# Attention probabilities left undivided, with the reciprocal sums brought into the gate by way of memory

## The chip, the cores and the metric

The kernel runs on one core of a Trainium2 chip. Times are microseconds of the device for one execution. The engines are named as in the profile: PE is TensorE's matmuls, PEld its weight loads, DVE VectorE, ACT ScalarE, POOL GpSimd, and SP SyncE, which here issues all DMAs, one after the other, on a single queue.

## The reference, cut to what matters

One encoder layer over 4096 tokens of 1024 channels: a combined projection, windowed attention (8 query heads, 2 key heads, 64 channels each) beside a pooling branch, both gated, an output projection, and a norm with a residual. Of it, the change concerns the softmax and what follows it:

```python
qb = q.reshape(B, nb, BLOCK, N_KV_HEADS, Q_PER_KV, HEAD_DIM)
...
s = jnp.where(valid[None, :, None, None], s + bias[None, None], NEG)
m = jnp.maximum(jnp.max(s, axis=-1, keepdims=True), sk)
p = jnp.exp(s - m)
p = p / (jnp.sum(p, axis=-1, keepdims=True) + jnp.exp(sk - m))
o = jnp.einsum('bnkgqs,bnskd->bnqkgd', p.astype(v.dtype), vw)
...
a = banded_attention(q, k, v, rel_bias, attn_sink[l]) * jax.nn.silu(g_a)
...
mixed = jnp.einsum('bse,ed->bsd', jnp.concatenate([a, p], axis=-1), w_out[l])
```

A block has 128 queries and sees up to 384 keys: its own block and the two beside it. `sk` is a sink logit that counts in the sum and has no value.

## The kernel before

The program has two stages. The first, to about 475 us, projects the two gates and the pooling input for all tokens, in units of 512 tokens, and leaves them in DRAM. The second, which the change touches, walks the 32 blocks from the last to the first. For each unit of two blocks (256 tokens) it projects keys, values and queries, runs the attention of both blocks, multiplies it with the gate, and projects the result. Every float32 number that a matmul reads is carried as a pair of float16 numbers, a high part and the rest, so each product takes three matmuls.

A block b is handled in two **halves** of four heads. The steps of a half, with their functions:

- `scores`: PE writes four heads' scores into two PSUM tiles, `s0` and `s1`.
- `logits`, four times on DVE: adds the bias, finds the maximum, and writes the float32 tile `p` in SBUF. Its first call also has POOL copy the sink logits into the last column of `p` (the small COPY of `nsink`).
- `exps`, four times on ACT: the exponential in place, with the sum of a row into `den`. Its first call waits for that copy.
- `denominators` on DVE: scales `den` and takes the reciprocal `rd`.
- `probs`, four times on ACT: the probability p times rd, as the high float16 part `pn`; `rests`, four times on DVE: the rest.
- `turn`: one transposing DMA on SP that turns `pn` into `pt`, keys on the partitions.

When both halves are there, `values` has PE multiply `pt` with the values, and `gate` has DVE multiply the result with the gate tile `gb` (`ga_t[b]`, loaded from DRAM by `load_ga`). The names `y11`, `y12`, `y22`, `ys1` to `ys4` are the seven operands of the output projection of a unit; each is cast on ACT (`high`) and gets its rest on POOL (`low`).

What sets the order is written out by hand: each step is put into a list with a due time in us by `due` or `at_`, the list is sorted by that time, and each engine gets its instructions in the sorted order. An engine works through its own list strictly in that order: an instruction that waits holds up all behind it. The first four blocks and the last two have tables of times (`soft` and `at_`); blocks 27 to 2 are planned by a loop that takes an odd block and then the even one below it, 13 times. In the loop `softmax(b, half, t)` places a half's steps from the time t at which its scores are planned to be there.

Three queues matter for the steps below. On PE the odd part of the loop runs, in order, scores (b, 0), one output product, keys and values of the next unit, `values` of the block before, scores (b, 1), and four output products (`m22`, `m11`, `ms2`, `m12`); the even part runs scores (b, 0), queries of the next unit (first `aq`), `values`, scores (b, 1), queries (second `aq`), and two output products. The two query products use one PSUM bank in turn, so the second starts only when `keep_q` has emptied the first: a high part on ACT (`q`), then the rest on DVE. In the same way `m22` uses the bank that `keep_k` and `keep_v` (`k_all`, `vs`) have to empty.

Of the kernel before, what the change touches and what calls it, by code (L numbers as in the profile page):

```python
# [8 lines left out]
F32 = mybir.dt.float32  # L9
# [3 lines left out]
AF = mybir.ActivationFunctionType  # L13
ALU = mybir.AluOpType
# [39 lines left out]
P_SCALE = 2.0**14  # L54
# [80 lines left out]
def hybrid_layer(ctx: ExitStack, tc, io, out):  # L135
    nc = tc.nc
# [43 lines left out]
    x_scr = dram.tile([NU, P, 2, 2, HK, UT], F16, name="x_scr")  # L180
    yp_scr = dram.tile([NB, P, 4, P], F32, name="yp_scr")
    ga_scr = dram.tile([NB, P, 4, P], F32, name="ga_scr")
    wb_scr = dram.tile([6, P, 2, D], F16, name="wb_scr")
    w_scr = dram.tile([8, P, 2, HK, 512], F16, name="w_scr")

# [25 lines left out]
    with ExitStack() as actx:  # L211
# [13 lines left out]
        rows = pa.tile([P, T], F32, name="rows")  # L225
# [9 lines left out]
        def turn(name):  # L235
            turns[name] += 1
            return turns[name] % 2
# [716 lines left out]
        b = turn("n2")  # L954
        for j in range(4):
            ld(9.5 + 0.1 * j, wut[:, j], io["w_uT"][j], 0.5, w=[f"wut{j}"])
            z = turn("sq")
            for half in range(2):
                t = U0 + 4 * j + 2 * half
# [245 lines left out]
        g = 0  # L1205
# [29 lines left out]
    pb = ctx.enter_context(tc.tile_pool(name="pb", bufs=2, reuse_waits="tile"))  # L1235
    pb1 = ctx.enter_context(tc.tile_pool(name="pb1", bufs=1, reuse_waits="tile"))
# [40 lines left out]
                n += 1  # L1277

    pt, p_t, nm_t, den_t, rd_t, pn_t = {}, {}, {}, {}, {}, {}

    def keys(b):
        return [kb for kb in range(3) if 0 <= b - 1 + kb < NB]
# [6 lines left out]
    def due(t, fn, *args):  # L1289
        plan.append((t, len(plan), fn, args))  # L1290
# [30 lines left out]
    def logits(b, half, i):  # L1321

        kbs = keys(b)
        nk, lo, j0 = len(kbs) * P, kbs[0] * P, 2 * half
        if i == 0:
            nm_t[b, half] = pb.tile([P, 4], F32, name=f"nm{b}_{half}", tag="nm")
            den_t[b, half] = pb.tile([P, 4], F32, name=f"den{b}_{half}", tag="den")
            rd_t[b, half] = pb.tile([P, 4], F32, name=f"rd{b}_{half}", tag="rd")
            p = p_t[b, half] = pb.tile([P, 4, 3 * P + 1], F32, name=f"p{b}_{half}", tag="p")
            nc.gpsimd.tensor_copy(  # L1330
                p.rearrange("p (g j) k -> p g j k", g=2)[:, :, :, nk],
                nsink.rearrange("p (g j) -> p g j", g=2)[:, :, j0 : j0 + 2],
            )
        jj, gg = divmod(i, 2)
        hh, h = 2 * gg + jj, 4 * gg + j0 + jj
        nc.vector.tensor_tensor_reduce(  # L1336
            out=p_t[b, half][:, hh, :nk], in0=s_t[jj][:, gg, :nk],
            in1=bias[:, h, lo : lo + nk], scale=negc[:, h : h + 1], scalar=nsink[:, h : h + 1],
            op0=ALU.add, op1=ALU.min, accum_out=nm_t[b, half][:, hh : hh + 1],
        )  # L1340

    def exps(b, half, i):
        nk = len(keys(b)) * P
        jj, gg = divmod(i, 2)
        hh = 2 * gg + jj
        p = p_t[b, half]
        nc.scalar.activation(  # L1347
            p[:, hh, : nk + 1], p[:, hh, : nk + 1], AF.Exp, bias=nm_t[b, half][:, hh : hh + 1],
            scale=-1.0, accum_out=den_t[b, half][:, hh : hh + 1],
        )  # L1350

    def denominators(b, half):
        den = den_t.pop((b, half))
        nc.vector.tensor_scalar(
            out=den, in0=den, scalar1=1.0 / P_SCALE, scalar2=None, op0=ALU.mult
        )
        nc.vector.reciprocal(rd_t[b, half], den)

    def prob_view(b, half):
        nk = len(keys(b)) * P  # L1360
        return pn_t[b, half][:, : 8 * nk].rearrange("p (v h k) -> p v h k", v=2, h=4)

    def probs(b, half, i):
        nk = len(keys(b)) * P
        if i == 0:
            pn_t[b, half] = pb.tile(
                [P, 2 * 4 * 3 * P], F16, name=f"pn{b}_{half}", tag="pn", bufs=PN_BUFS
            )
        nc.scalar.activation(  # L1369
            prob_view(b, half)[:, 0, i], p_t[b, half][:, i, :nk], AF.Copy,  # L1370
            scale=rd_t[b, half][:, i : i + 1],
        )

    def rests(b, half, i):
        nk = len(keys(b)) * P
        pn4 = prob_view(b, half)
        nc.vector.scalar_tensor_tensor(  # L1377
            out=pn4[:, 1, i], in0=p_t[b, half][:, i, :nk], scalar=rd_t[b, half][:, i : i + 1],
            in1=pn4[:, 0, i], op0=ALU.mult, op1=ALU.subtract,
        )  # L1380

    def turn(b, half):
# [6 lines left out]
    def softmax(b, half, t):  # L1389

        for i in range(4):
            due(t + 0.1 + 0.67 * i, logits, b, half, i)
            due(t + 0.8 + 0.8 * i, exps, b, half, i)
            due(t + 4.5 + 0.6 * i, probs, b, half, i)
            due(t + 5.1 + 0.62 * i, rests, b, half, i)
        due(t + 4.3, denominators, b, half)
        due(t + 7.8, turn, b, half)


    kv_t = {}  # L1400
# [55 lines left out]
    ga_t, o_t = {}, {}  # L1456
# [244 lines left out]
    def load_gain():  # L1701
        nc.sync.dma_start(
            gpost, io["g_post"].rearrange("(o a) -> o a", o=1).to_broadcast([P, D])
        )

    now = [0.0]
    dummy = pb1.tile([P, 1], F32, name="dummy")

# [9 lines left out]
    def visit(b, half):  # L1718
        now[0] = max(now[0], free[0])
        t = max(pe(1.1, scores, b, half), free[1])  # L1720
        softmax(b, half, t)
        free[:] = t + 2.9, t + 7.9
# [71 lines left out]
    def at_(t, fn, *args):  # L1794
        due(z + t, fn, *args)

    def soft(b, half, tl, te, td, tp, tr, tt):

        for i in range(4):
            at_(tl + 0.62 * i, logits, b, half, i)  # L1800
            at_(te + 0.65 * i, exps, b, half, i)
            at_(tp + 0.55 * i, probs, b, half, i)
            at_(tr + 0.62 * i, rests, b, half, i)
        at_(td, denominators, b, half)
        at_(tt, turn, b, half)

    def cast(th, tw, u, name, f, eng):
# [11 lines left out]
    for t, fn, *args in (  # L1819
# [33 lines left out]
        at_(t, fn, *args)  # L1853

    soft(NB - 1, 0, 14.2, 14.6, 17.0, 17.6, 18.0, 20.1)
    soft(NB - 1, 1, 20.6, 21.1, 23.7, 24.2, 24.6, 26.5)
    soft(NB - 2, 0, 27.2, 27.8, 31.1, 31.6, 32.2, 34.5)
    soft(NB - 2, 1, 34.4, 35.0, 38.3, 38.8, 39.4, 41.7)
    soft(NB - 3, 0, 42.0, 42.6, 45.9, 46.4, 47.0, 49.3)
    soft(NB - 3, 1, 50.1, 50.7, 54.0, 54.5, 55.1, 57.4)  # L1860
    soft(NB - 4, 0, 59.4, 60.0, 63.2, 63.7, 64.3, 67.0)
    softmax(NB - 4, 1, 67.6)

    at_(0.0, lambda: nc.scalar.activation(dummy, mhalf, AF.Exp))
# [280 lines left out]
```

## Time and profile before

| | |
|---|---|
| median of 3 runs | 1165.77 us (1164.74 to 1165.78) |
| the profiled execution's own time | 1163.94 us |
| its span on the core | 1162.2 us |
| mean granted clock of TensorE | 0.997 |
| DMA | 228.36 MB, mean 196 GB/s |

The span runs from the first to the last instruction of the program; the execution's own time has 1.7 us more around it. All durations below come from this one execution. In the timeline a row gives the start, the duration, the engine, the line, the operation, and what was written and read; in brackets stands how long the engine had been idle and what ended that. A repeated row carries its count.

### The profile page before, as it was taken

The numbers are of one execution on the slowest core, as the hardware profiler recorded it, in microseconds if no ns is written. First come the engines' busy times: TensorE is split into PE (matmuls) and PEld (weight loads), VectorE is DVE, ScalarE is ACT, GpSimd is POOL, SyncE is SP. The second block draws the span as 40 slices with busy tenths as digits, with TensorE's granted clock in tenths as the row PEclk, the third lists the DMA queues.
The fourth block names the chain that finished last, engine by engine and source line by source line (L and its number), as shares of the span: only waits on it lengthen the run. The fifth ranks groups of instructions, "written<-read, shape, count | busy, mean of one in ns | idle before, by whom it ended". The sixth has DMA issues, their size and how long they took to land. (4 is left out here: it accounts for less than half of the span.)

```text
span 1162.2 us, 32275 instructions
## 1 busy us (share of the span) xinstructions
PE 1146.4 (99%) x13420; PEld 873.9 (75%) x13420; DVE 936.7 (81%) x1875; ACT 701.9 (60%) x1460; POOL 314.9 (27%) x310
## 2 busy tenths in 40 slices
PE   8999999999999999999999999999999999999997
PEld 6998888888888888886667576676666767667653
DVE  6889988988799973568878877877787887787786
ACT  6876546546654542267666676666667667666772
POOL 0002121211111010201524433533542443353231
PEclk9999999999999999999999999999999999999999
DMA  9645585867667764299986887787787788776785
GB/s 342 219 127 182 173 272 180 283 219 251 213 191 234 209 168 132 85 284 254 233 198 141 205 200 148 201 194 183 165 196 185 152 207 200 142 200 158 179 213 143
DMA packets 301683, 228.36 MB, mean 196 GB/s; under 512 B 219568, under 2 KB 259504, under 8 KB 296928
## 3 DMA queue, kind: packets, MB, share of 16 engines
q1 hardware_dynamic: 301536, 226.30, 72.5%
q8 instruction: 105, 1.72, 0.6%
q14 instruction: 42, 0.34, 0.1%
HBM read 114.68 MB, written 60.34 MB: 151 GB/s over the span
## 5 line engine op out<-in xcount | busy, mean ns | idle before, releaser
L689 PEld LDWEIGHTS <-wq 128*128 128x128 f16 x4104 | 401.6, 98 | 51.0 <-DVE wq L310 2.9
L689 PE MATMUL y<-xt,wq 128*128 128x256 f16 x1512 | 203.3, 273 | 0.1
L1347 ACT ACTIVATE p<-p,nm 128x385 f32<-128x385 f32 (+1 forms) x256 | 152.9, 599 | 36.4 <-POOL p L1330 20.4
L1273 PE MATMUL aq<-xb,xb 128*128 128x256 f16 x1024 | 173.4, 273 | 0.3 <-DVE mo L1668 0.3
L1273 PEld LDWEIGHTS <-xb 128*128 128x128 f16 x1536 | 150.2, 98 | 26.4 <-issue 8.0
L1629 PE MATMUL ms<-wo,ys 128*128 128x512 f16 x720 | 162.7, 379 | 0.0
L1377 DVE SCALAR_TENSOR_TENSOR pn<-p,rd,pn 128x384 f16<-128x384 f32 (+1 forms) x256 | 157.4, 666 | 5.9 <-ACT pn L1369 5.9
L1336 DVE CUSTOM_DVE_ANT_0 p<-s,nt,nsink 128x384 f32<-128x384 f32 (+1 forms) x256 | 156.0, 666 | 1.7 <-PE s L1313 1.7
L1273 PE MATMUL aq<-xb,xt 128*128 128x256 f16 x512 | 139.6, 273 | 0.2 <-issue 0.2
L1369 ACT ACTIVATE pn<-p,rd 128x384 f16<-128x384 f32 (+1 forms) x256 | 134.5, 596 | 4.0 <-issue 1.1
L307 POOL TENSOR_TENSOR yt<-yt,sg 128x512 f32<-128x512 f32 (+2 forms) x32 | 51.0, 1595 | 301.6 <-DVE yt L310 232.2
L1629 PEld LDWEIGHTS <-ys 128*128 128x128 f16 x720 | 69.1, 98 | 81.8 <-issue 3.6
L1629 PE MATMUL m<-wo,y 128*128 128x512 f16 x540 | 121.8, 379 | 0.0
L1629 PEld LDWEIGHTS <-y 128*128 128x128 f16 x540 | 51.5, 98 | 63.5 <-issue 3.6
L1663 POOL TENSOR_TENSOR mo<-mo,gpost 128x512 f32<-128x512 f32 x39 | 63.8, 1637 | 93.9 <-ACT jkb L1652 92.7
L1273 PE MATMUL kv<-xb,xb 128*128 128x256 f16 x512 | 86.7, 273 | 0.0
L1273 PEld LDWEIGHTS <-xt 128*128 128x128 f16 x768 | 75.2, 98 | 10.5 <-issue 0.8
L689 PE MATMUL plain<-xb,wq 128*128 128x256 f16 x576 | 67.8, 275 | 2.7 <-DVE wq L310 2.3
L1273 PE MATMUL kv<-xb,xt 128*128 128x256 f16 x256 | 69.8, 273 | 0.0
L689 PE MATMUL v<-xt,wq 128*128 128x256 f16 x504 | 68.6, 273 | 0.1
L689 PE MATMUL v<-xb,wq 128*128 128x256 f16 x504 | 68.6, 273 | 0.0
L689 PE MATMUL y<-xb,wq 128*128 128x256 f16 x504 | 68.6, 273 | 0.0
(215 smaller groups left out, 1830.1 us busy)
## 6 DMA issues: line engine op xcount, KB each, us to landing
nt<-in_xT SPq DMA_DIRECT2D x28, 512.0 KB
x_scr<-xb SPq DMA_DIRECT2D x14, 1024.0 KB
xb<-x_scr SPq DMA_DIRECT2D x14, 1024.0 KB
xr<-in_x SPq DMA_DIRECT2D x28, 512.0 KB
out<-xr SPq DMA_DIRECT2D x28, 512.0 KB
xn<-in_x SPq DMA_DIRECT2D x27, 512.0 KB
ga_scr<-cc SPq DMA_DIRECT2D x64, 128.0 KB
raw<-in_w_out SPq DMA_DIRECT2D x16, 512.0 KB
```

Of the source, the lines that this page charges most:

```text
L307: eng.tensor_tensor(out=out, in0=in0, in1=in1, op=op)
L689: nc.tensor.matmul(b[:, s], wq[:, slot[q, op], wv, s, k, :], x[:, xv, k, :], start=(first and k + s + wv + xv == 0), stop=(last and k == H ...
L1273: nc.tensor.matmul(acc, w[:, j, k, :], x[:, kh, v, kt, :], start=(n == 0), stop=(n == 3 * KT - 1),)
L1336: nc.vector.tensor_tensor_reduce(out=p_t[b, half][:, hh, :nk], in0=s_t[jj][:, gg, :nk], in1=bias[:, h, lo : lo + nk], scale=negc[:, h : h ...
L1347: nc.scalar.activation(p[:, hh, : nk + 1], p[:, hh, : nk + 1], AF.Exp, bias=nm_t[b, half][:, hh : hh + 1], scale=-1.0, accum_out=den_t[b, ...
L1369: nc.scalar.activation(prob_view(b, half)[:, 0, i], p_t[b, half][:, i, :nk], AF.Copy, scale=rd_t[b, half][:, i : i + 1],)
L1377: nc.vector.scalar_tensor_tensor(out=pn4[:, 1, i], in0=p_t[b, half][:, i, :nk], scalar=rd_t[b, half][:, i : i + 1], in1=pn4[:, 0, i], op0= ...
L1629: nc.tensor.matmul(z_t[u, tag], y[:, k, yi, :], wo[o][:, wi, k, :], start=(n == 0 and acc is None), stop=(n == 3 * HK - 1), skip_group_che ...
L1663: eng.tensor_tensor(out=mo, in0=mo, in1=gpost[:, cs], op=ALU.mult)
```

## The change

`denominators` is no longer on the way from the exponentials to the transposing DMA. `probs` and `rests` multiply with the constant `P_SCALE` in place of the reciprocal, and since that is the same number for all rows, one operation takes two heads (768 columns a row in place of 384), so that there are two of each a half in place of four. The division is made after the values: when both halves of a block have their sums (`den` now has 8 columns for a block), DVE takes the reciprocals into `rec0` and turns them in blocks of 32 by 32 into `rec1`; four small DMAs write them to DRAM as rows of 128 queries (`keep_rows`); two DMAs read each head's row back, the same for 64 partitions, into a spare part of the tile `xb0` (`load_rows`, 256 KB together); and POOL multiplies the gate tile with it (`divide`), before `gate` uses that tile.

```diff
+    rec = [pb1.tile([P, 32], F32, name=f"rec{i}") for i in range(2)]
+    rdb = XB0[:, 6 * D :].bitcast(F32).rearrange("p (i h q) -> p i h q", i=2, h=4)
...
-    def denominators(b, half):
-        den = den_t.pop((b, half))
-        nc.vector.tensor_scalar(
-            out=den, in0=den, scalar1=1.0 / P_SCALE, scalar2=None, op0=ALU.mult
-        )
-        nc.vector.reciprocal(rd_t[b, half], den)
+    def denominators(b):
+        nc.vector.reciprocal(rec[0][:, :NH], den_t.pop(b))
+        nc.vector.transpose(out=rec[1], in_=rec[0])
+
+    def keep_rows(b):
+        for i in range(4):
+            nc.sync.dma_start(
+                rd_scr[b, :, 32 * i : 32 * i + 32], rec[1][32 * i : 32 * i + NH, :]
+            )
+
+    def load_rows(b):
+        for g in range(2):
+            rows = rd_scr[b, 4 * g : 4 * g + 4, :].rearrange("(o h) q -> o h q", o=1)
+            nc.sync.dma_start(
+                rdb[64 * g : 64 * g + 64, b % 2], rows.to_broadcast([64, 4, P])
+            )
+
+    def divide(b):
+        ga = ga_t[b]
+        nc.gpsimd.tensor_tensor(out=ga, in0=ga, in1=rdb[:, b % 2], op=ALU.mult)
...
-        nc.scalar.activation(
-            prob_view(b, half)[:, 0, i], p_t[b, half][:, i, :nk], AF.Copy,
-            scale=rd_t[b, half][:, i : i + 1],
-        )
+        hs = slice(2 * i, 2 * i + 2)
+        nc.scalar.mul(prob_view(b, half)[:, 0, hs], p_t[b, half][:, hs, :nk], P_SCALE)
...
-            out=pn4[:, 1, i], in0=p_t[b, half][:, i, :nk], scalar=rd_t[b, half][:, i : i + 1],
-            in1=pn4[:, 0, i], op0=ALU.mult, op1=ALU.subtract,
+            out=pn4[:, 1, hs], in0=p_t[b, half][:, hs, :nk], scalar=P_SCALE,
+            in1=pn4[:, 0, hs], op0=ALU.mult, op1=ALU.subtract,
...
-            due(t + 4.5 + 0.6 * i, probs, b, half, i)
-            due(t + 5.1 + 0.62 * i, rests, b, half, i)
-        due(t + 4.3, denominators, b, half)
-        due(t + 7.8, turn, b, half)
+        for i in range(2):
+            due(t + 4.1 + 0.75 * i, probs, b, half, i)
+            due(t + 5.0 + 0.95 * i, rests, b, half, i)
+        if half:
+            due(t + 4.3, denominators, b)
+            due(t + 4.9, keep_rows, b)
+            due(t + 8.0, load_rows, b)
+            due(t + 11.0, divide, b)
+        due(t + 6.9, turn, b, half)
...
+            at_(td, denominators, b)
+            at_(td + 0.4, keep_rows, b)
+            at_(max(tt + 0.1, td + 2.5), load_rows, b)
+            at_(max(tt + 2.6, td + 5.0), divide, b)
```

The change moves instructions in three queues. They are shown for one passage of the loop, the odd block 17 and the even block 16. A name ends in its block and half (`p16_0` is half 0 of block 16) or its unit (`ys4_9` is unit 9) and a running number.

GpSimd's queue, from the rest of `ys1` of unit 9; first before, then after:

```order
L1535 TENSOR_TENSOR ys1_9_11765<-s1_9_11669,ys1_9_11765 128x4x128
L1535 TENSOR_TENSOR ys4_9_11820<-yf1_9_11109,ys4_9_11820 128x4x128
L1330 COPY p16_0_11875<-nsink_87 128x4
L1330 COPY p16_1_12086<-nsink_87 128x4
L1535 TENSOR_TENSOR y11_8_12032<-at17_11975,y11_8_12032 128x4x128
L1663 TENSOR_TENSOR mo9_1_11716<-mo9_1_11716,gpost_6084 128x512
L1330 COPY p15_0_12213<-nsink_87 128x4
L1663 TENSOR_TENSOR mo9_1_11716<-mo9_1_11716,gpost_6084 128x512
```

```order
L1557 TENSOR_TENSOR ys1_9_11678<-s1_9_11582,ys1_9_11678 128x4x128
L1375 TENSOR_TENSOR gb17_11527<-gb17_11527,xb0_66 128x512
L1557 TENSOR_TENSOR ys4_9_11733<-yf1_9_11034,ys4_9_11733 128x4x128
L1333 COPY p16_0_11788<-nsink_87 128x4
L1333 COPY p16_1_11991<-nsink_87 128x4
L1557 TENSOR_TENSOR y11_8_11939<-at17_11884,y11_8_11939 128x4x128
L1685 TENSOR_TENSOR mo9_1_11629<-mo9_1_11629,gpost_6085 128x512
L1375 TENSOR_TENSOR gb16_11995<-gb16_11995,xb0_66 128x512
L1333 COPY p15_0_12120<-nsink_87 128x4
```

The product for block 17 (`gb17`, L1375) now stands ahead of the rest of `ys4` and of the sink copy for the first half of block 16, and the product for block 16 ahead of the sink copy for the first half of block 15.

SyncE's queue from the transposing DMA of block 17's second half (`pt17_1`) to a little behind that of block 16's second half; first before, then after:

```order
L1386 DMA_TRANSPOSE pt17_1_11746<-pn17_1_11721 128x24x128
L1558 DMA yf0_8_11761<-yp_scr_96 128x512
L1558 DMA yf1_8_11880<-yp_scr_96 128x512
L1386 DMA_TRANSPOSE pt16_0_12026<-pn16_0_11892 128x24x128
L1676 DMA xr18_12028<-in_x 128x1024
L1676 DMA xr19_12030<-in_x 128x1024
L1460 DMA gb16_12090<-ga_scr_97 128x512
L1259 DMA xb1_68<-x_scr_95 128x4096
L1386 DMA_TRANSPOSE pt16_1_12129<-pn16_1_12104 128x24x128
L1696 DMA out_0<-xr18_12028 128x1024
```

```order
L1403 DMA_TRANSPOSE pt17_1_11657<-pn17_1_11626 128x24x128
L1369 DMA xb0_66<-rd_scr_98 64x512 x2
L1580 DMA yf0_8_11674<-yp_scr_96 128x512
L1580 DMA yf1_8_11793<-yp_scr_96 128x512
L1403 DMA_TRANSPOSE pt16_0_11882<-pn16_0_11800 128x24x128
L1698 DMA xr18_11935<-in_x 128x1024
L1698 DMA xr19_11937<-in_x 128x1024
L1482 DMA gb16_11995<-ga_scr_97 128x512
L1362 DMA rd_scr_98<-rec1_6088 8x32 x4
L1403 DMA_TRANSPOSE pt16_1_12033<-pn16_1_12004 128x24x128
L1260 DMA xb1_68<-x_scr_95 128x4096
L1369 DMA xb0_66<-rd_scr_98 64x512 x2
```

The writes of the sums' rows (`rd_scr<-rec1`) stand ahead of a block's second transposing DMA, and the loads of the rows (`xb0<-rd_scr`) behind it, right behind in the odd block; in the even block the 1 MB load of the next unit's operand (`xb1`) has changed places with the transposing DMA and stands between it and the rows.

ScalarE's queue at the first half of block 16; first before, then after:

```order
L1531 CAST ys4_9_11820<-yf1_9_11109 128x4x128
L1347 ACTIVATE p16_0_11875,den16_0_11873<-p16_0_11875,nm16_0_11872 128x385 x4
L1262 ACTIVATE q7_0_11889<-aq7_0_11822 128x512
L1369 ACTIVATE pn16_0_11892<-p16_0_11875,rd16_0_11874 128x384 x4
L1531 CAST y11_8_12032<-at17_11975 128x4x128
```

```order
L1553 CAST ys4_9_11733<-yf1_9_11034 128x4x128
L1350 ACTIVATE p16_0_11788,den16_11787<-p16_0_11788,nm16_0_11786 128x385 x4
L1388 ACTIVATE pn16_0_11800<-p16_0_11788 128x768
L1263 ACTIVATE q7_0_11802<-aq7_0_11736 128x512
L1388 ACTIVATE pn16_0_11800<-p16_0_11788 128x768
```

One of the two operations of `probs` now stands ahead of `q7_0`, the high part of the queries, which all four stood behind before; the exponentials are ahead of it in both.

More of the change, by code (lines that the diff above doesn't have):

```diff
@@ L182, in hybrid_layer @@
     ga_scr = dram.tile([NB, P, 4, P], F32, name="ga_scr")
+    rd_scr = dram.tile([NB, NH, P], F32, name="rd_scr")
     wb_scr = dram.tile([6, P, 2, D], F16, name="wb_scr")
@@ L1326, in logits @@
             nm_t[b, half] = pb.tile([P, 4], F32, name=f"nm{b}_{half}", tag="nm")
-            den_t[b, half] = pb.tile([P, 4], F32, name=f"den{b}_{half}", tag="den")
-            rd_t[b, half] = pb.tile([P, 4], F32, name=f"rd{b}_{half}", tag="rd")
+            if half == 0:
+                den_t[b] = pb.tile([P, NH], F32, name=f"den{b}", tag="den")
             p = p_t[b, half] = pb.tile([P, 4, 3 * P + 1], F32, name=f"p{b}_{half}", tag="p")
@@ L1348, in exps @@
             p[:, hh, : nk + 1], p[:, hh, : nk + 1], AF.Exp, bias=nm_t[b, half][:, hh : hh + 1],
-            scale=-1.0, accum_out=den_t[b, half][:, hh : hh + 1],
-        )
-    def denominators(b, half):
-        den = den_t.pop((b, half))
-        nc.vector.tensor_scalar(
-            out=den, in0=den, scalar1=1.0 / P_SCALE, scalar2=None, op0=ALU.mult
-        )
-        nc.vector.reciprocal(rd_t[b, half], den)
+            scale=-1.0,
+            accum_out=den_t[b][:, 4 * gg + 2 * half + jj : 4 * gg + 2 * half + jj + 1],
+        )
+    def denominators(b):
[15 more added lines that the diff above has]
+        nc.gpsimd.tensor_tensor(out=ga, in0=ga, in1=rdb[:, b % 2], op=ALU.mult)
     def prob_view(b, half):
@@ L1376, in rests @@
         pn4 = prob_view(b, half)
+        hs = slice(2 * i, 2 * i + 2)
         nc.vector.scalar_tensor_tensor(
-            out=pn4[:, 1, i], in0=p_t[b, half][:, i, :nk], scalar=rd_t[b, half][:, i : i + 1],
-            in1=pn4[:, 0, i], op0=ALU.mult, op1=ALU.subtract,
+            out=pn4[:, 1, hs], in0=p_t[b, half][:, hs, :nk], scalar=P_SCALE,
+            in1=pn4[:, 0, hs], op0=ALU.mult, op1=ALU.subtract,
         )
@@ L1704, in load_gain @@
         )
+    due(-1.0, nc.vector.memset, rec[0], 0.0)
     now = [0.0]
@@ L1801, in soft @@
             at_(te + 0.65 * i, exps, b, half, i)
-            at_(tp + 0.55 * i, probs, b, half, i)
-            at_(tr + 0.62 * i, rests, b, half, i)
-        at_(td, denominators, b, half)
+        for i in range(2):
+            at_(tp + 0.8 * i, probs, b, half, i)
+            at_(tr + 0.95 * i, rests, b, half, i)
+        if half:
+            at_(td, denominators, b)
+            at_(td + 0.4, keep_rows, b)
+            at_(max(tt + 0.1, td + 2.5), load_rows, b)
+            at_(max(tt + 2.6, td + 5.0), divide, b)
         at_(tt, turn, b, half)
```

## The prediction

> **What bounds the kernel now.** I read the page first, then TensorE's waits, the busy times of one stretch, and the timeline of each queue in it.
>
> ```profile
> PE 1146.4 (99%) x13420; PEld 873.9 (75%) x13420; DVE 936.7 (81%) x1875; ACT 701.9 (60%) x1460; POOL 314.9 (27%) x310
> ...
> PE o L1479 <- DMA pt<-pn: 1.1, 2, 0.7
> ...
> PE z L1601 <- DVE xb L1668: 0.6, 1, 0.6
> ...
> PE aq L1273 <- DVE mo L1668: 0.3, 1, 0.3
> ...
> 780.00:822.00 42.00, 42.00 (x588) 28.31 (x584) 34.00 (x80) 27.56 (x69) 17.19 (x18) 1.00 0.80 180
> ```
>
> TensorE is the bound: 1146.4 of 1162.2 us, and in the middle of the second stage 42.00 of 42.00. The three waits are nearly all that it has there, 1.1 + 0.6 + 0.3 = 2.0 us, and that is the most that a shorter softmax can save. The change leaves TensorE's work as it is. So the question is whether the new chain stays ahead of TensorE. I follow block 17 (odd) and block 16 (even).
>
> ```profile
> 792.38 3.67 SPq L1386 DMA_TRANSPOSE pt<-pn  x1
> 796.14 1.02 SPq L1558 DMA_DIRECT2D yf<-yp_scr  x2
> ...
> 808.14 0.42 SPq L1259 DMA_DIRECT2D xb<-x_scr  x1
> 812.52 5.23 SPq L1386 DMA_TRANSPOSE pt<-pn  x1
> ...
> 833.96 3.59 SPq L1386 DMA_TRANSPOSE pt<-pn  x1
> ```
>
> The rows at 792.38 and 833.96 are the same transposing DMA one passage of the loop apart: a passage takes 41.6 us. SyncE is held for some 3.6 us by each such DMA, and nothing behind it is issued before that ends.
>
> **The change part by part.** What is removed or made larger, first.
>
> ```profile
> 788.64 0.17 DVE L1354 TENSOR_SCALAR den<-den 128x4 f32<-128x4 f32 x1 [0.84 <-ACT p L1347]
> ...
> 788.94 1.27 DVE L1690 SCALAR_TENSOR_TENSOR xr<-mo,rs,xr 128x1024 f32<-128x1024 f32 x1
> 789.11 2.13 ACT L1369 ACTIVATE pn<-p,rd 128x384 f16<-128x384 f32 x4
> 790.12 2.20 DVE L1377 SCALAR_TENSOR_TENSOR pn<-p,rd,pn 128x384 f16<-128x384 f32 x4
> ...
> L319 ACT ACTIVATE xn<-xn 128x1024 f32<-128x1024 f32 x27 | 28.4, 1052 | 0.0
> ...
> L455 DVE STREAM_TRANSPOSE turned<-turned x5: 211/211/214, 142.8 to 339.9; 128x32 f32<-128x32 f32 x5
> ...
> L459 SPq DMA_DIRECT2D rs_scr<-turned x20: 483/485/602, 143.1 to 341.7; - x20
> ```
>
> Four rests take 2.20 us, 0.55 each at 384 columns; 1024 columns take 1.27. Between them, 768 come to about 0.98, two to 1.95: 0.25 us less. Four probs take 2.13, 0.53 each; 1024 columns take 1.05, so 768 lie between; I take 0.80. None of this is on TensorE's path, so I credit it with nothing. Nor does it bring block 17's transposing DMA forward: there VectorE's `den` step is replaced by a transposition (0.21), the residual (1.27) still stands ahead of the rests, and the last rest ends at 788.64 + 0.2 + 0.2 + 1.3 + 1.95 = 792.3, as before. The four row writes (4 x 0.485 = 1.94 us on SyncE) fit between 789.1 and 792.3, where SyncE waits for the rests anyway; without that cover the transposing DMA would start up to 1.94 later.
>
> *Odd block: the product on GpSimd.* It needs the rows, and they are issued behind the transposing DMA.
>
> ```profile
> 199.63 0.39 SPq L466 DMA_DIRECT2D rows<-rs_scr  x1
> ...
> 202.94 2.18 POOL L307 TENSOR_TENSOR yt<-yt,sg 128x512 f32<-128x512 f32 x1 [4.76 <-DMA rows<-rs_scr]
> ...
> 528.66 4.04 SPq L1386 DMA_TRANSPOSE pt<-pn  x1
> ...
> 535.83 0.25 PE L1479 MATMUL o<-pt,vv 128*64 128x128 f16 x2 [0.74 <-DMA pt<-pn]
> ...
> L1573 POOL TENSOR_TENSOR yf<-yf,at 128x512 f32<-128x512 f32 x15 | 19.2, 1277 | 0.9 <-DVE at L1570 0.9
> ...
> L1663 POOL TENSOR_TENSOR mo<-mo,gpost 128x512 f32<-128x512 f32 x39 | 63.8, 1637 | 93.9 <-ACT jkb L1652 92.7
> ...
> 795.10 1.17 POOL L1535 TENSOR_TENSOR ys<-yf,ys 128x512 f16<-128x512 f32 x1
> 796.21 0.32 POOL L1330 COPY p<-nsink 128x4 f32<-128x4 f32 x2
> ...
> 796.43 0.62 ACT L1347 ACTIVATE p<-p,nm 128x385 f32<-128x385 f32 x1 [1.41 <-POOL p L1330]
> ...
> 799.31 0.60 ACT L1262 ACTIVATE q<-aq 128x512 f16<-128x512 f32 x1 [0.37 <-PE aq L1273]
> ...
> 799.94 0.69 DVE L1263 SCALAR_TENSOR_TENSOR q<-aq,q 128x512 f16<-128x512 f32 x1 [0.58 <-ACT q L1262]
> ...
> 801.98 0.28 PE L1273 MATMUL aq<-xb,xb 128*128 128x256 f16 x1
> ```
>
> SyncE is free at 796.05; the two row loads take the place of the pair at 796.14 (1.02 us), the second starting near 796.6. A broadcast load of this size landed 202.94 - 199.63 = 3.3 us after its issue: 799.9. A transposing DMA landed 535.83 - 528.66 = 7.2 after its start: 799.6 here, with the rows' 256 KB behind it. So the rows land at 799.5 to 800.8; I take 800.0. GpSimd's product of 128x512 lies between 1.28 and 1.64; 1.5 gives 801.5. What is queued behind it on GpSimd: the rest of `ys4` (1.17) and the sink copy (0.2), to 802.9. For the copy ScalarE's exponentials wait, and they did already before: their row says 1.41 us for POOL. They start 6.5 us late, at 802.9 in place of 796.43. Behind them on ScalarE stand four exponentials (2.5 us, to 805.4), one `probs` (0.80) and the high part of the queries (0.60), to 806.8; then VectorE's rest (0.69), to 807.5. For that the second query product waits, since it uses the same bank. It started at 801.98, so TensorE stands still for **5.5 us** (4.5 with the low ends of rows, product and `probs`, 6.7 with the high ends).
>
> *Even block.* All of VectorE's and ScalarE's work between that point and the second transposing DMA follows as before, so I leave this distance as it was, T - 801.98 = 10.5 with T = 812.52.
>
> ```profile
> GB/s 342 219 127 182 173 272 180 283 219 251 213 191 234 209 168 132 85 284 254 233 198 141 205 200 148 201 194 183 165 196 185 152 207 200 142 200 158 179 213 143
> ...
> 814.03 0.62 ACT L1347 ACTIVATE p<-p,nm 128x385 f32<-128x385 f32 x1
> ...
> 816.95 0.63 ACT L1652 ACTIVATE jkb<-mo 128x512 bf16<-128x512 f32 x1 [0.41 <-DVE mo L1668]
> ...
> 819.61 1.12 ACT L1531 CAST y<-yf 128x512 f16<-128x512 f32 x2
> 821.41 0.38 ACT L1262 ACTIVATE k_all<-kv 128x256 f16<-128x256 f32 x1 [0.68 <-PE kv L1273]
> ...
> 823.08 0.42 DVE L1263 SCALAR_TENSOR_TENSOR vs<-kv,vs 128x256 f16<-128x256 f32 x1 [0.45 <-ACT vs L1262]
> ...
> 824.08 0.82 PE L1629 MATMUL m<-wo,y 128*128 128x512 f16 x3
> ```
>
> After T the queue issues the transposing DMA (to T + 3.7), the 1 MB load (0.42) and the rows (the second at T + 4.7). By their own 3.3 us they land at T + 8.0. Behind the transposing DMA (T + 7.2), the 1 MB at the page's best rate, 342 GB/s (3.1), and their own 256 KB (0.8) they land at T + 11.1. That what stands ahead counts, the trace shows: the transposing DMA right behind the 1 MB load took 5.23 to issue, against 3.59. I take T + 10.0, nearer to the upper end since the first term of it includes a completion that following data need not wait for. [...]
>
> From T + 10.0: product 1.5, sink copy 0.25, exponentials 2.5, one square 0.6, two `probs` 1.6, two casts 1.1, that is T + 17.5; then keys and values leave their bank, from the row at 821.41 to the end of that at 823.08, 2.1 us: T + 19.6. The output product that needs the bank started at 824.08 = T + 11.56. TensorE stands still for **8.1 us** (5.4 with the low ends, 9.8 with the high).
>
> The two add up, since the even chain starts from the query product that the odd one delays, and the next odd chain from the output product that the even one delays; the slack, 1.4 and 0.6 us in these rows, is spent in each.
>
> *TensorE after standing still.* The trace shows the price once.
>
> ```profile
> 18.50:20.00 1.50, 1.41 (x7) 1.04 (x8) 1.50 (x4) 1.49 (x3) 0.00 (x0) 0.50 1.06 424
> ...
> 18.59 2.53 PE L689 MATMUL plain<-xb,wq 128*128 128x256 f16 x11 [2.35 <-DVE wq L310]
> ```
>
> After 2.35 us without work, in a loosely filled stretch, the granted clock was 0.50. Some 3.4 us at half rate lose 1.7. After the output product's wait TensorE has 5 us in hand again before the next wait, which hide it; after the query product's wait it delays the second half of the queries and with it T. I take 0.6 us a passage.
>
> **Sum.** 5.5 + 8.1 + 0.6 = 14.2 us a passage. The loop makes 13: the odd chain occurs for blocks 27 to 3, the even one for 28 to 4 (block 2's product stands behind the next copy). 13 x 14.2 = 185 us. The tables add little: in the first blocks sink copies come 1 to 3 us late (TensorE already waits 1.1 there), and at the end the last product holds a mean on GpSimd, a residual on VectorE and the last gate; 3 us each, my estimate, 6 in all. From the execution's own 1163.94: 1355 us. The median of the runs shown is 1.8 us higher, which is nothing against the range.
>
> **The rivals.**
> *The rows are there in time (faster).* If the product on GpSimd ended before the rest of `ys4` is due (795.1), it would hold up nothing; the rows would have to land by 793.6, and the planned times (rows 3.0 us before the product) mean just that. Then the 2.0 us of waits are the gain: 1162 us. Against it: SyncE's row at 792.38, behind which they are issued. 4 in 100, with 2 in 100 for no difference.
> *Only one chain bites.* If the rows of the even block pass by the load ahead, or the banks have more room than the rows say, the odd chain alone is left: 13 x 5.5 = 72, 1237 us. 8 in 100.
> *Half rate after every stand-still.* If both restarts lose 1.7 us that nothing hides, 2.8 more a passage: 36 us, 1391 us. For it: the row with 0.50 after only 2.35 us. Against it: the time in hand. 14 in 100. [...]
> That the change does not do what it says I leave at nothing: the product and the loads stand in the queues.
>
> **How the numbers follow.** Forecast, both chains: 72 in 100, 1355 us. Low ends: 13 x 9.9 = 129, 1293 us; high ends with the clock: 13 x (16.5 + 3.4) = 259, 1423 us. The range 1290 to 1423 leaves out the first two rivals, 14 in 100, and a little beyond its ends. Slower by over 0.2% (about what a measurement of this kernel can tell from no change): 0.94; within: 0.02; faster: 0.04.
>
> **What would show it.** In the profile after: a passage of about 56 us between the same transposing DMAs; TensorE waiting twice in it, `aq` for VectorE's `q` by some 5 us and the output product `m` for VectorE's `vs` by some 8; GpSimd waiting for the row loads ahead of each product, and ScalarE's first exponential for GpSimd by 6 us and more; the granted clock below 1 in these stretches. It would be wrong if GpSimd hardly waits for the rows, or if TensorE waits for something else, such as `pt`.

## The result, and the profile after

The changed kernel takes 1372.18 us (median of 4 runs, 1367.42 to 1375.26), against 1165.26 of the kernel before beside it: a ratio of 1.178, with a 95% interval of 1.1763 to 1.1799. The prediction was 1355 us, between 1290 and 1423. The profiled execution took 1367.42 us, its span 1365.6.

First the page: the busy times, the granted clock in 40 slices, and four of its groups (busy time, mean ns of one, then the idle time ahead of them and what ended most of it).

```profile
PE 1199.6 (88%) x13420; PEld 894.7 (66%) x13420; DVE 901.2 (66%) x1684; ACT 661.8 (48%) x1332; POOL 336.9 (25%) x342
...
PEclk9999999999999999988999889998899988999899
...
L1350 ACT ACTIVATE p<-p,nm 128x385 f32<-128x385 f32 (+1 forms) x256 | 152.8, 598 | 243.4 <-POOL p L1333 230.2
L1274 PE MATMUL aq<-xb,xb 128*128 128x256 f16 x1024 | 196.5, 294 | 52.0 <-DVE q L1264 49.8
L1651 PE MATMUL m<-wo,y 128*128 128x512 f16 x540 | 148.1, 437 | 93.1 <-DVE vs L1264 91.2
...
L1375 POOL TENSOR_TENSOR gb<-gb,xb 128x512 f32<-128x512 f32 x32 | 40.9, 1278 | 209.4 <-DMA xb<-rd_scr 199.2
```

From the bottom to the top, the groups say this: GpSimd waits 199.2 us for the rows ahead of its products, ScalarE 230.2 us for GpSimd's sink copies ahead of the exponentials, and TensorE 49.8 us for the low part of the queries and 91.2 us for that of the values. TensorE's 13420 matmuls, as many as before, take 53.2 us longer (1199.6 against 1146.4): the granted clock averages 0.941 over the span, 0.997 before, and all slices that show an 8 (below nine tenths) lie in the second stage.

One passage of the loop, in the timeline of SyncE, GpSimd, ScalarE and TensorE (start, duration, then the instruction, in brackets the idle time before it):

```profile
771.17 3.61 SPq L1403 DMA_TRANSPOSE pt<-pn  x1
774.97 1.10 SPq L1369 DMA_DIRECT2D xb<-rd_scr  x2
...
798.17 3.65 SPq L1403 DMA_TRANSPOSE pt<-pn  x1
801.92 0.54 SPq L1260 DMA_DIRECT2D xb<-x_scr  x1
802.63 1.09 SPq L1369 DMA_DIRECT2D xb<-rd_scr  x2
...
827.40 3.71 SPq L1403 DMA_TRANSPOSE pt<-pn  x1
...
778.97 1.28 POOL L1375 TENSOR_TENSOR gb<-gb,xb 128x512 f32<-128x512 f32 x1 [4.20 <-DMA xb<-rd_scr]
...
808.13 1.27 POOL L1375 TENSOR_TENSOR gb<-gb,xb 128x512 f32<-128x512 f32 x1 [7.31 <-DMA xb<-rd_scr]
...
781.53 0.62 ACT L1350 ACTIVATE p<-p,nm 128x385 f32<-128x385 f32 x1 [6.69 <-POOL p L1333]
...
809.56 0.62 ACT L1350 ACTIVATE p<-p,nm 128x385 f32<-128x385 f32 x1 [8.92 <-POOL p L1333]
...
786.02 0.37 PE L1274 MATMUL aq<-xb,xb 128*128 128x256 f16 x1 [4.16 <-DVE q L1264]
...
817.15 7.66 PE L1651 MATMUL m<-wo,y 128*128 128x512 f16 x24 [6.48 <-DVE vs L1264]
```

The passage, from one odd transposing DMA to the next, takes 827.40 - 771.17 = 56.2 us in place of 41.6. The odd product starts 7.8 us after its transposing DMA, the even one 10.0 us after; each time ScalarE's exponential follows GpSimd, and TensorE's wait follows that. The 24 output products take 7.66 us.

To place the whole difference I cut the span at two transposing DMAs that both kernels have: that of block 28's second half, and, 13 passages later, that of block 2's. Their rows, in the kernel before and in the changed one:

```profile
562.85 6.41 SPq L1386 DMA_TRANSPOSE pt<-pn  x1
...
1101.74 6.07 SPq L1386 DMA_TRANSPOSE pt<-pn  x1
```

```profile
572.83 5.88 SPq L1403 DMA_TRANSPOSE pt<-pn  x1
...
1302.39 4.96 SPq L1403 DMA_TRANSPOSE pt<-pn  x1
```

Up to the first cut 10.0 us are lost, in the 13 passages 190.7 (729.6 against 538.9), behind the second 2.7: together the 203.4 us between the spans. The kernels of the experiments, described below, are cut in the same way, each at the same two DMAs of its own profiled execution. The last three columns give the difference to the kernel before in us.

| kernel | median us | start | 13 passages | end |
|---|---|---|---|---|
| before | 1165 | 0 | 0 | 0 |
| changed | 1372.2 | +10.0 | +190.7 | +2.7 |
| no_division | 1162.1 | -0.9 | -0.4 | -0.5 |
| no_product | 1170.1 | +7.5 | +0.4 | -2.2 |
| late_odd | 1300.7 | +13.0 | +124.4 | +3.8 |
| late_even | 1301.1 | +11.9 | +120.7 | +4.6 |
| late_both | 1202.2 | +10.0 | +22.2 | +3.9 |
| rows_before_x | 1342.7 | +11.7 | +164.4 | +2.4 |
| rows_first | 1241.9 | +12.7 | +62.8 | +1.3 |
| filled | 1363.4 | +11.0 | +183.8 | +2.1 |
| filled2 | 1358.3 | +10.7 | +176.5 | +3.6 |
| placed | 1184.2 | +9.6 | +12.7 | -1.7 |
| placed2 | 1189.7 | +15.1 | +13.9 | -2.1 |
| placed3 | 1183.2 | +11.0 | +12.2 | -1.2 |

### The profile page after: what moved, and what is told of

It is laid out like the page before. It is cut to its first block, busy times and chain, and to the rows that moved or that the text cites. A ratio compares the mean times of both kernels' runs of the same rounds, so it can differ in the third digit from the quotient of the medians.

```text
span 1365.6 us, 32282 instructions
## 1 busy us (share of the span) xinstructions
PE 1199.6 (88%) x13420; PEld 894.7 (66%) x13420; DVE 901.2 (66%) x1684; ACT 661.8 (48%) x1332; POOL 336.9 (25%) x342
## 5 line engine op out<-in xcount | busy, mean ns | idle before, releaser
L1350 ACT ACTIVATE p<-p,nm 128x385 f32<-128x385 f32 (+1 forms) x256 | 152.8, 598 | 243.4 <-POOL p L1333 230.2
L1274 PE MATMUL aq<-xb,xb 128*128 128x256 f16 x1024 | 196.5, 294 | 52.0 <-DVE q L1264 49.8
L1651 PE MATMUL m<-wo,y 128*128 128x512 f16 x540 | 148.1, 437 | 93.1 <-DVE vs L1264 91.2
L1274 PEld LDWEIGHTS <-xb 128*128 128x128 f16 x1536 | 158.0, 103 | 34.7 <-issue 8.0
L1274 PE MATMUL aq<-xb,xt 128*128 128x256 f16 x512 | 150.8, 295 | 0.0
L1394 DVE SCALAR_TENSOR_TENSOR pn<-p,pn 128x768 f16<-128x768 f32 (+1 forms) x128 | 124.6, 1004 | 19.8 <-ACT pn L1388 19.8
L1264 DVE SCALAR_TENSOR_TENSOR q<-aq,q 128x512 f16<-128x512 f32 x31 | 21.4, 692 | 143.5 <-ACT q L1263 143.5
L1712 DVE SCALAR_TENSOR_TENSOR xr<-mo,rs,xr 128x1024 f32<-128x1024 f32 x28 | 35.5, 1266 | 109.2 <-POOL rs L1708 109.0
L1388 ACT ACTIVATE pn<-p 128x768 f16<-128x768 f32 (+1 forms) x128 | 102.3, 817 | 0.0
L1375 POOL TENSOR_TENSOR gb<-gb,xb 128x512 f32<-128x512 f32 x32 | 40.9, 1278 | 209.4 <-DMA xb<-rd_scr 199.2
L1685 POOL TENSOR_TENSOR mo<-mo,gpost 128x512 f32<-128x512 f32 x39 | 49.5, 1269 | 127.3 <-ACT jkb L1674 127.3
```

The source lines that it names most:

```text
L1264: nc.vector.scalar_tensor_tensor(out=dst_l, in0=acc, scalar=QKV_EVAC, in1=dst_h, op0=ALU.mult, op1=ALU.subtract)
L1274: nc.tensor.matmul(acc, w[:, j, k, :], x[:, kh, v, kt, :], start=(n == 0), stop=(n == 3 * KT - 1),)
L1350: nc.scalar.activation(p[:, hh, : nk + 1], p[:, hh, : nk + 1], AF.Exp, bias=nm_t[b, half][:, hh : hh + 1], scale=-1.0, accum_out=den_t[b][ ...
L1375: nc.gpsimd.tensor_tensor(out=ga, in0=ga, in1=rdb[:, b % 2], op=ALU.mult)
L1388: nc.scalar.mul(prob_view(b, half)[:, 0, hs], p_t[b, half][:, hs, :nk], P_SCALE)
L1394: nc.vector.scalar_tensor_tensor(out=pn4[:, 1, hs], in0=p_t[b, half][:, hs, :nk], scalar=P_SCALE, in1=pn4[:, 0, hs], op0=ALU.mult, op1=ALU ...
```

## The experiments

All start from the changed kernel, and the ratios are to the kernel before, with their 95% intervals. Theory A is that of the prediction: the product, waiting on GpSimd's queue, holds up what stands behind it there, and two chains end in waits of TensorE.

**Which part costs: no_product and no_division.** The first takes only the product away, the second every part of the division.

```diff
-            due(t + 11.0, divide, b)
...
-            at_(max(tt + 2.6, td + 5.0), divide, b)
```

> The reciprocals are written and the rows loaded as in the changed kernel, but the product on GpSimd is left out, so the output is not divided by the sums. Theory A: the transfers alone cost nothing that shows, 1160 to 1170 us. Rival B (the transfers themselves) or C (SyncE's queue): above 1300 us, near 1372.

```diff
-        if half:
-            due(t + 4.3, denominators, b)
-            due(t + 4.9, keep_rows, b)
-            due(t + 8.0, load_rows, b)
-            due(t + 11.0, divide, b)
...
-        if half:
-            at_(td, denominators, b)
-            at_(td + 0.4, keep_rows, b)
-            at_(max(tt + 0.1, td + 2.5), load_rows, b)
-            at_(max(tt + 2.6, td + 5.0), divide, b)
```

> The division is left out altogether: no reciprocals, row writes, loads or product; what remains of the change is the undivided probabilities made for two heads per operation, and their earlier place. Theory A: TensorE sets the time as before, 1160 to 1167 us, no difference from the kernel before of more than 0.3%. Rival C (the two-head operations delay the transposing DMA): 1175 us or above.

Without the product: 1170.13 us (1.0057, 1.0042 to 1.0072). Without the division: 1162.12 us (0.9984, 0.9970 to 0.9997). The rows are still written and loaded in the first, and the passages take what they took before (+0.4 us over all 13), so neither the transfers nor SyncE's extra work costs anything there that shows: rivals B and C fall for the loop. What the transfers do cost is 7.5 us at the start, where TensorE waits for transposed probabilities, and then works at a lower clock (from 526 to 555 us its page shows an 8 for the granted clock, below nine tenths); in its waits, and in the rows of VectorE and SyncE ahead of the longer one:

```profile
PE o L1500 <- DMA pt<-pn: 5.9, 2, 3.9
...
523.35 2.79 DVE L1394 SCALAR_TENSOR_TENSOR pn<-p,pn 128x768 f16<-128x768 f32 x2
...
522.39 6.18 SPq L1403 DMA_TRANSPOSE pt<-pn  x1
...
531.68 4.81 SPq L1403 DMA_TRANSPOSE pt<-pn  x1
```

The rests were ready at 526.1 us, but SyncE, held by the transposing DMA ahead, two loads and the row writes, came to theirs only at 531.68.

The half of the change that makes undivided probabilities for two heads at once is harmless, and on its own about 0.2% faster, which is at the edge of what these runs tell apart.

**Which chain costs what: late_both, late_odd, late_even.** The product keeps its rows but is put further back on GpSimd, shortly ahead of its gate; with both, with odd blocks only, with even blocks only.

```diff
-            due(t + 11.0, divide, b)
+            due(t + (17.5 if b % 2 else 20.5 if b > 2 else 11.0), divide, b)
```

> The product on GpSimd stands behind the sink copy, the gains and the casts of the next block, shortly ahead of its own gate; nothing else is changed. Theory A (the waiting product holds up GpSimd's queue, above all the sink copy): both waits of TensorE in the loop are gone, 13 x 14.6 us come back, about 1165 to 1175 us, what is left above the kernel before being the tables at both ends. Rival B (the rows' transfers crowd out other transfers) or C (the two-head operations or SyncE's extra work are what is slow): the time stays above 1300 us.

> Only the product of odd blocks stands late. Theory A: the wait of the second query product is gone, the one of the output product for VectorE's vs stays at some 7 us with a half clock of some 2 us behind it; 13 x 9 = 118 us above the kernel before and some 7 for the tables: 1290 us, 1270 to 1305. Rival B or C: no change, 1372 us.

> Only the product of even blocks stands late. Theory A: the output product no longer waits, the second query product still does, 3.8 to 5.3 us with some 2 us of half clock behind it; 13 x 5.9 to 7.3 and some 7 for the tables: 1250 to 1270 us. Rival B or C: no change, 1372 us.

Measured: 1202.18 (1.0326, 1.0311 to 1.0341), 1300.72 (1.1180) and 1301.11 us (1.1178). TensorE's longest waits in late_odd and in late_even are these:

```profile
PE m L1651 <- DVE vs L1264: 90.0, 13, 7.6
```

```profile
PE aq L1274 <- DVE q L1264: 71.9, 13, 6.1
```

Each removes its own wait and leaves the other, so the two chains are there, and they are separate. Late_odd came out as expected. Late_even was expected at 1250 to 1270 and took 1301: its remaining wait is 5.5 us (71.9 / 13) in place of 3.8, since the query product starts as late behind its transposing DMA as in the changed kernel (15.1 and 15.0 us on average) and TensorE, not slowed ahead of it (the matmuls of the output products `m` take 386 ns each on average, 437 in the changed kernel), is there earlier; and the new place of the even product costs something of its own. The savings do not add up either: over the passages late_odd saves 66.3 us, late_even 70.0, and late_both 168.5. So a chain left alone costs more than its share of the two together. Late_both, expected at 1165 to 1175, took 1202; the cost of the new places shows in it, 22.2 us over the passages:

```profile
796.75 0.55 POOL L1708 TENSOR_TENSOR rs<-ms,mhalf 128x1 f32<-128x1 f32 x1 [1.95 <-DVE ms L1703]
797.27 2.27 POOL L1557 TENSOR_TENSOR y<-yf,y 128x512 f16<-128x512 f32 x2
799.51 1.26 POOL L1375 TENSOR_TENSOR gb<-gb,xb 128x512 f32<-128x512 f32 x1
...
800.80 0.48 DVE L1525 SCALAR_TENSOR_TENSOR at<-o,gaf,gb 128x256 f32<-128x256 f32 x1 [2.92 <-POOL gb L1375]
...
805.80 2.33 PE L1651 MATMUL ms<-wo,ys 128*128 128x512 f16 x10 [0.63 <-POOL ys L1557]
```

The product no longer waits for its rows, but it stands behind a mean and two rests, and the gate waits 2.92 us for it. Placed late, it moved the wait to the next reader.

**Whether the megabyte ahead counts: rows_before_x.**

```diff
-            due(t + 8.0, load_rows, b)
+            due(t + 7.2, load_rows, b)
```

> In even blocks the two row loads are issued ahead of the 1 MB load of the next unit, still behind the transposing DMA. Theory A1 (the rows' data stands behind the megabyte on the DMA engines): the rows land some 2.5 to 3 us earlier, the product and the output product's wait follow, 13 x 2.5 to 2.9 us: 1335 to 1340 us. Rival A2 (their own latency, 3.3 us, is what counts, the megabyte does not): about 1370 us.

Measured: 1342.69 us (1.1521, 1.1501 to 1.1541), 29.5 less than the changed kernel.

```profile
794.75 3.65 SPq L1403 DMA_TRANSPOSE pt<-pn  x1
798.58 1.09 SPq L1369 DMA_DIRECT2D xb<-rd_scr  x2
...
802.12 1.27 POOL L1375 TENSOR_TENSOR gb<-gb,xb 128x512 f32<-128x512 f32 x1 [4.74 <-DMA xb<-rd_scr]
```

The product starts 7.4 us after the transposing DMA instead of 10.0. Of these 2.6 us the loads gain 0.6 by their earlier issue (798.58 - 794.75 = 3.8 us after the transposing DMA, in place of 802.63 - 798.17 = 4.5). So the rows did stand behind the megabyte's data, by about 2.0 us, where the prediction had taken 3.1 from the best rate of the page.

**Whether the rows can come first: rows_first.**

```diff
-            due(t + 8.0, load_rows, b)
+            due(t + 6.0, load_rows, b)
```

> The row loads are issued right behind the row writes, ahead of the transposing DMA; SyncE then waits for the writes to land. Theory A: in odd blocks the rows are there some 5 us earlier, before GpSimd reaches the product, and the query product no longer waits; in even blocks the writes land 4 us after their issue, so the transposing DMA starts some 1 us later and the rows some 6 us earlier, which leaves 1 to 3 us of wait a passage: 1185 to 1215 us. Rival: the transposing DMA behind a waiting SyncE becomes the new bound, both blocks lose 3 us and more: 1250 us or above.

Measured: 1241.86 us (1.0659, 1.0642 to 1.0676). Better than the changed kernel, but beyond what I expected. An even block, then an odd one, on SyncE, and TensorE behind the latter:

```profile
755.35 1.06 SPq L1698 DMA_DIRECT2D xr<-in_x  x2
756.46 0.43 SPq L1482 DMA_DIRECT2D gb<-ga_scr  x1
756.93 1.34 SPq L1362 DMA_DIRECT2D rd_scr<-rec  x4
762.22 1.09 SPq L1369 DMA_DIRECT2D xb<-rd_scr  x2
763.42 3.73 SPq L1403 DMA_TRANSPOSE pt<-pn  x1
...
782.14 1.29 SPq L1362 DMA_DIRECT2D rd_scr<-rec  x4
784.32 1.10 SPq L1369 DMA_DIRECT2D xb<-rd_scr  x2
...
786.87 5.00 SPq L1403 DMA_TRANSPOSE pt<-pn  x1
...
795.43 0.25 PE L1501 MATMUL o<-pt,vv 128*64 128x128 f16 x2 [2.80 <-DMA pt<-pn]
```

The loads must wait for the writes to land, and SyncE waits with them: 4.0 us in the even block (758.27 to 762.22), 0.9 in the odd one (783.43 to 784.32). The transposing DMA behind it starts late and, in the odd block, takes 5.00 us. TensorE has a new wait for `pt`, in 16 places, and a part of the old one for VectorE's `vs` is left:

```profile
PE m L1651 <- DVE vs L1264: 28.1, 13, 3.2
PE o L1501 <- DMA pt<-pn: 19.9, 16, 2.8
```

The rival's mechanism is there too, then, at a smaller price than it was given.

**What the halved clock costs: filled and filled2.** Extra matmuls, whose result nothing reads, stand ahead of the two instructions that wait (in filled 110 of them ahead of the output product and 50 ahead of the second query product, in filled2 110 and 90).

```diff
+    def fill(n):
+        for _ in range(n):
+            nc.tensor.matmul(
+                s_t[0][:, 0, 3 * P : 4 * P], wb_h[:, 0, 0, :], wb_h[:, 0, 1, :],
+                start=True, stop=True, skip_group_check=True,
+            )
...
             visit(b, 1)
+            due(now[0], fill, 110)
             mix_p4(u + 1)
...
             visit(b, 1)
+            due(now[0], fill, 50)
             do_q(u - 1, 1)
```

> The changed kernel with TensorE kept busy in most of both waits by extra matmuls (50 ahead of the second query product, 110 ahead of the output product) into columns of a PSUM bank that nothing reads. Theory A with the clock in the chain: the granted clock stays at 1, and 13 x 2.0 us come back: about 1346 us (1335 to 1355). By the prediction's step (the halved clock after the output product's wait is hidden by time in hand) 13 x 0.6: 1364 us. Rival (the waits absorb it all): 1372 us.

> As filled, with 90 instead of 50 extra matmuls ahead of the second query product, so that no halving is left in the loop. If the halved clock costs only what is not hidden (the step of the prediction, 0.6 us a passage in all): 1355 to 1364 us. If the halvings that filled left over cost their full 1.7 us each: 1348 us or below.

Measured: 1363.40 us (1.1715, 1.1694 to 1.1737) and 1358.29 us (1.1657, 1.1639 to 1.1674). From filled2's page, its busy times, its clock, and the extra matmuls:

```profile
PE 1305.2 (96%) x16020; PEld 1020.8 (75%) x16020; DVE 898.7 (66%) x1684; ACT 659.9 (49%) x1332; POOL 339.2 (25%) x342
...
PEclk9999999999999999999999999999999999999999
```

```profile
L1292 PE MATMUL s<-xb 128*128 128x128 f16 x2600 | 149.7, 219 | 0.0
```

And from filled's timeline, the 24 output products that took 7.66 us in the changed kernel, here with TensorE kept busy up to 0.32 us before them:

```profile
819.30 5.47 PE L1658 MATMUL m<-wo,y 128*128 128x512 f16 x24 [0.32 <-DVE vs L1264]
```

At a granted clock of 1.00 (the average from 820 to 880 us) they take 5.47. In filled2, without the extra matmuls, TensorE is busy for 1305.2 - 149.7 = 1155.5 us, 44 less than in the changed kernel. The time falls by 13.9. So about two thirds of what the slower clock adds to TensorE's own work is hidden: a TensorE that is slower between two waits arrives later at the next, and waits there less. The net price is 13.9 / 13 = 1.1 us a passage, or a little more, as in three of 26 places the extra matmuls run past the end of the wait, by 3.0 us together. Both times lie where the prediction's step, a clock that is mostly hidden, put them; a clock that costs its full loss (1346 us for filled, 1348 or below for filled2) is out.

**Can it be made to pay: placed, placed2, placed3.** Placed combines what worked: rows ahead of the megabyte, the odd product as in late_both, the even one between GpSimd's last gain and its mean, and the tables' products shortly ahead of their gates.

```diff
-            due(t + 8.0, load_rows, b)
-            due(t + 11.0, divide, b)
+            due(t + 7.2, load_rows, b)
+            due(t + (17.5 if b % 2 else 17.0 if b > 2 else 16.3), divide, b)
...
-            at_(max(tt + 2.6, td + 5.0), divide, b)
+            at_({NB - 1: 37.0, NB - 2: 52.0, NB - 3: 65.5, 1: 33.0, 0: 43.0}[b], divide, b)
```

> Rows of even blocks ahead of the 1 MB load; the product late on GpSimd's queue: in odd blocks behind the sink copy as in late_both, in even blocks between the second gain and the second mean, where GpSimd waited some 2 us for the mean anyway; in the tables shortly ahead of each gate. Theory A: the 1.75 us a passage that late_both still loses (its even product stands behind two casts, so the gate is late) are gone, the passage is 41.6 us, and what stays is some 5 us of waits for pt at the start of the second stage: 1165 to 1173 us. Rival (the product of even blocks costs at any place): 1185 us or above.

Placed2 issues the first two blocks' rows later, placed3 leaves them and issues four large loads of the start later.

```diff
-            at_(max(tt + 0.1, td + 2.5), load_rows, b)
+            at_({NB - 1: 34.6, NB - 2: 49.4}.get(b, max(tt + 0.1, td + 2.5)), load_rows, b)
```

> placed, and for the first two blocks the row loads behind the next transposing DMA, so that SyncE does not stand waiting for row writes that lie behind a 512 KB load. Theory A: some 3 to 5 us less than placed, 1162 to 1168 us, no longer to be told from the kernel before. Rival (the waits for pt at the start have another cause): as placed.

```diff
-    at_(20.3, load_wo, O21)
-    at_(26.6, load_wo, OT2)
-    at_(36.5, load_x, U - 3)
-    at_(41.8, load_wo, OT3)
+    at_(26.7, load_wo, O21)
+    at_(42.0, load_wo, OT3)
+    at_(42.1, load_wo, OT2)
+    at_(50.5, load_x, U - 3)
```

> placed, and at the start of the second stage four large loads (three of 512 KB, one of 1 MB) behind the row writes, the transposing DMA and the row loads in place of ahead of them. Theory A (SyncE stands waiting for row writes whose data lies behind these loads, and every transposing DMA behind it is late): the 8.9 us of waits of TensorE at the start fall to 2 or 3, 1176 to 1180 us. Rival (the start is late for another reason): as placed, 1184 us.

Measured: 1184.24 (1.0160, 1.0146 to 1.0173), 1189.71 (1.0211) and 1183.17 us (1.0164). All three missed. In placed TensorE's waits for VectorE's low parts are gone but for 0.2 us at a time. Yet the passages still cost 12.7 us: 4.0 of it are two waits in the first one, 1.8 for `pt` and 2.1 for a rest of GpSimd's, and behind these no single wait of TensorE in the passages is above 0.7 us. The start still costs 9.6, half of it one wait for `pt`; in placed3 that wait has only moved to a later transposing DMA:

```profile
540.34 0.32 PE L1501 MATMUL o<-pt,vv 128*64 128x128 f16 x2 [5.02 <-DMA pt<-pn]
```

```profile
557.10 0.32 PE L1501 MATMUL o<-pt,vv 128*64 128x128 f16 x2 [6.44 <-DMA pt<-pn]
```

Moving the large loads only chose which of the transposing DMAs is late. In placed2, whose start costs 15.1, the rows come too late instead: the gate waits up to 8.5 us for the product, and TensorE 6.3 for the gate. Whether the start can be ordered so that nothing is late, and what the other 8.7 us of the passages, 0.7 each, consist of, stays open. No version that divides beats the kernel before.

## Why the prediction was right, and where it was off

- **The bound, and what the change can save.** Right. With the division gone TensorE is the bound as before, and the whole saving is 2.4 us (no_division against the 1164.54 beside it), close to the 2.0 us of waits that the prediction read off. One reading beside it did not hold: the shorter softmax does bring the odd block's transposing DMA forward, from 9.8 us behind the output product to 9.4 in no_product, on average; but TensorE does not wait for it there.
- **The odd chain.** Right in each link, and to 0.3 us. Rows: taken at 7.6 us behind the transposing DMA's start, the product started at 7.8. Exponentials: taken at 10.5 (802.9 - 792.38), they started at 10.36. The second query product: taken at 15.1 (9.6 + 5.5), it started at 14.85. Late_odd shows that this chain is the product's doing.
- **The even chain.** Right. Product taken at T + 10.0, started at T + 9.96; exponentials taken at T + 11.75, started at T + 11.4; output product taken at T + 19.7, started at T + 19.0. The step that was least certain, rows behind the megabyte, held, as rows_before_x shows, though at 2.0 us and not 3.1; the choice of T + 10.0 between the ends, 8.0 and 11.1, fell well. Data behind the transposing DMA did move before the 7.2 us taken for its landing were over: the DMAs' rate, 208 GB/s from 799.25 to 802.75 us, was 453 from 804.25 to 805.37, which is T + 6.1 to T + 7.2.
- **What TensorE stands still.** The prediction called the two delays, 5.5 and 8.1 us, time in which TensorE stands still. The delays are real: in the passages shown the query product starts 14.85 us behind its transposing DMA in place of 9.60, and the output product 18.98 in place of 11.56, so 5.25 and 7.42 us later; on average over the 13 passages it is 5.3 and 7.7. But TensorE's waits are shorter, 3.8 and 7.0 us (49.8 and 91.2 over 13), since a part of each delay is filled by TensorE's slower work ahead of the wait, not by idleness.
- **The clock: mis-sized.** The step "Some 3.4 us at half rate lose 1.7", with most of it hidden, gave 0.6 us a passage. The loss at each restart is larger: 24 output products take 7.66 us, with the granted clock at 0.50 from 817 to 821 us, and 5.47 where the clock stays up (filled), 2.2 us less. Most of it is indeed hidden, as was argued, but 1.1 us a passage is not. The rows show where: from the delayed product to the next transposing DMA it takes 10.25 us (827.40 - 817.15) in place of 9.88 behind the output product, and 12.15 (798.17 - 786.02) in place of 10.54 behind the query product, 2.0 more together and 1.6 on average, where the prediction had 0.6. What the average has beyond the clock's 1.1 is not traced further.
- **The sum.** In part luck. The two delays were taken 0.5 us a passage too large (13.6, measured 13.1 on average), the distances behind them 1.0 too small. So 185 us for the passages came within 6 of the 190.7 measured by two errors that partly cancel.
- **The tables: mis-sized.** 6 us were taken, 3 at each end. The end costs 2.7. The start costs 10.0, and no_product puts 7.5 of that down to the row writes and loads themselves, ahead of and between transposing DMAs that are then late. The prediction looked for late sink copies at the start and overlooked SyncE's queue, which it had checked in the loop only.
- **The rivals.** "The rows are there in time" fell with GpSimd's 199.2 us of waiting. "Only one chain bites" is what late_odd and late_even look like, not the changed kernel; its price of 1237 us was too low, since late_even, which leaves the odd chain alone, takes 1301, even if up to 22 of that are the product's new place. "Half rate after every stand-still", 1391 us, saw rightly that both restarts lose, but not that most of it is hidden. Placed is what comes nearest to the first rival: with the waits of the product gone, the change is still 1.6% slower.

Summed over the profiled execution, 185 became 190.7 and 6 became 12.7, which makes 1367.4 in place of 1355; the median of the four runs lies another 4.8 us above this execution.

## What to carry to other kernels

An instruction that waits costs what stands behind it on its engine, so when a step is added to an in-order queue, first list what is queued behind it and by when that is needed; here a 1.3 us product that waits for its rows cost 170 us more ahead of a 0.2 us copy than behind it (late_both). Moving it back is no cure by itself, since its reader then waits (2.92 us for the gate in late_both). And when an engine that sets the time has to wait, more busy time at a lower clock is not an equal loss: of the 44 us here 13.9 were paid, and the rest only filled the next wait.

## What the runs showed of the hardware

The clock can stay low for longer than the 3.4 us that the prediction took from the kernel before. Stretches of both kernels, with TensorE's busy time first, then the weight loads, VectorE, ScalarE and GpSimd, the granted clock, the DMA share and GB/s; first the kernel before, then the changed one:

```profile
17.50:18.50 1.00, 0.00 (x0) 0.00 (x0) 1.00 (x2) 1.00 (x2) 0.00 (x0) 0.83 1.06 367
18.50:20.00 1.50, 1.41 (x7) 1.04 (x8) 1.50 (x4) 1.49 (x3) 0.00 (x0) 0.50 1.06 424
20.00:21.50 1.50, 1.50 (x12) 1.19 (x10) 1.50 (x3) 0.95 (x2) 0.00 (x0) 0.50 1.04 426
21.50:23.00 1.50, 1.50 (x18) 1.37 (x16) 1.43 (x5) 0.72 (x2) 0.61 (x2) 0.98 1.01 412
```

```profile
782.00:786.00 4.00, 0.00 (x0) 0.00 (x0) 0.72 (x2) 3.98 (x11) 0.00 (x0) 0.79 0.19 66
786.00:790.00 4.00, 3.98 (x19) 2.82 (x19) 4.00 (x9) 1.44 (x4) 0.78 (x1) 0.50 0.28 53
790.00:791.00 1.00, 1.00 (x7) 0.72 (x5) 0.88 (x4) 1.00 (x5) 0.38 (x1) 0.50 1.16 218
```

In the kernel before, the clock is at 0.50 from 18.2 to 21.6 us. In the changed kernel's wait of 4.16 us it averages 0.79, so it is halved for the last 1.7 us of it (0.21 x 4 / 0.5), and it stays halved for 5 us of work after that: some 6.7 us in all, twice the 3.4. The trace has 26 such stretches in the second stage: 14 of 6.8 us, nine of 3.4 and three of 10.2, each one, two or three times 3.4. The halving begins some 2.5 us into this wait, and 1.9 us into the one of 2.35 us in the kernel before.

The four row writes of a block are 1 KB each. In rows_first SyncE waits 0.9 us for them, once issued, in the odd block, where the last load ahead was issued some 5 us earlier, and 4.0 us in the even block, where two loads of 512 KB and one of 256 KB had been issued within the last 1.6 us: the same small writes took longer behind loads issued shortly before.
